# Down products of the channel mixers by Strassen's seven products over quarters, with pools of weights that begin and end with each phase

## The chip, the core and the metric

The kernel runs on one NeuronCore of a Trainium2 chip, as one program that leaves its output in HBM. What counts is the device time of one execution in microseconds (us). Engines: TensorE multiplies matrices (PE in the profile, PEld its weight loads), VectorE (DVE) and ScalarE (ACT) do elementwise work, GpSimd (POOL) almost nothing here, SyncE (SP) issues the transfers from HBM. TensorE writes its sums into PSUM, eight banks of 128 x 512 fp32 values; everything else lies in SBUF.

## The reference

A trunk of two layers over 512 tokens of 1024 features, fp32. Layer 0 has a chunked gMLP as its mixer (mixer A), layer 1 an RG-LRU (mixer B); each is followed by a gated ConvFFN, the channel mixer, whose last line is what the change rewrites:

```python
def conv_ffn(h, w_up, conv_w, conv_b, w_down):
    up = causal_dwconv(h @ w_up, conv_w, conv_b)
    gate, val = jnp.split(up, 2, axis=-1)
    return (jax.nn.gelu(gate) * val) @ w_down

    for i in range(DEPTH):
        h = rms_norm(x, norm_mix[i])
        ...
        h = rms_norm(x, norm_ffn[i])
        x = x + conv_ffn(h, f_w_up[i], f_conv_w[i], f_conv_b[i], f_w_down[i])
    return rms_norm(x, norm_final)
```

`w_up` is 1024 x 6144, `w_down` 3072 x 1024, and the depthwise convolution has three taps along the tokens.

## The kernel before

Activations lie feature-major: a tile is 128 features by 512 tokens, and `xall` keeps the eight tiles of `x`. The kernel keeps fp32 accuracy by splitting every operand into a high part, rounded to TensorE's fp32r format, and the exact rest, the low part. A product is then three matmuls that add up in PSUM, high by high, high by low and low by high (`mm3`, L99 to 103).

**Weights.** They stream from HBM in chunks of 512 KB, that is two tiles of 128 input rows by 512 output columns, 1024 values a partition. `load` (L93) issues the transfer into a `raw` buffer, and `split` (L85) makes the parts: ScalarE copies `raw` into `hi` (L89), VectorE subtracts for `lo` (L90), both at high priority. `raw`, `hi` and `lo` have three buffers each. Chunk names end in r, h and l: `fu000r` is the raw chunk of the first ConvFFN's up weights, block 0, chunk 0; `fu1..` belongs to the second ConvFFN, `fd0w..` and `fd1w..` to the down products, `aow..` to the output product of mixer A, `bx..` to the input product of mixer B.

**Blocks.** `block` (L106) takes four PSUM tiles, one for each 128 output features, and runs through the chunks of a weight; a chunk meets 24 matmuls of 512 columns. The up product of a ConvFFN is 12 such blocks of four chunks each. After each, VectorE multiplies the four tiles by the norm's scale (`up`, L468), ScalarE and VectorE convolve them (`conv`, L442 to 448; one step on ScalarE, two on VectorE), GELU and the gate make two tiles `cv`, and `to_parts` (L238) leaves their parts as `fy..`. After the 12 blocks the 24 tiles `fy` are the input of the down product: two column blocks of 512 output features, 12 chunks each. In layer 0 this is `project` (L245), in layer 1 `project_out` (L256), which also does the final norm and takes the last two chunks by halves of the tokens, with matmuls of 256 columns. `project` adds each finished tile to `xall` (L250) and makes the next norm's input at once: `norm_input` (ScalarE makes `xh`, L198; VectorE makes `xl`, L199), `square` (ScalarE `sq`, L207; VectorE adds it to `acc`, L208). The norm's scale itself is found later, by hooks that run after the first chunks of the next block.

**What sets the order.** The code is written in program order, and a tile scheduler puts each engine's instructions into a queue by priority and by what they depend on. The engine then works through its queue in that order and waits at each instruction for what it needs. The pools of buffers (`const`, `wp` for weights, `yp` for activations, `wk` for work tiles, `pp` for PSUM) are opened once and stay open for the whole program (L49 to 53).

Of the kernel before, what the change touches and what calls it, by code (L numbers as in the profile page):

```python
# [30 lines left out]
# Columns of the packed per-channel vectors.  # L31
# [13 lines left out]
def trunk(ctx: ExitStack, tc: tile.TileContext, xT, vecs, a_w_in, a_w_sT, a_b_s, a_w_out,  # L45
# [11 lines left out]

    def work(name="w"):
        return wk.tile([P, S], F32, tag="w", name=name)

    def work_r(name="wr"):
        return wk.tile([P, S], F32R, tag="w", name=name)

    def yhi(name="yh"):
        return yp.tile([P, S], F32R, tag="yh", name=name)

    def ylo(name="yl"):
        return yp.tile([P, S], F32R, tag="yl", name=name)

    # Activations whose tables differ, in the order of the program.  # L70
# [13 lines left out]
    # A chunk of a weight: 1024 values a partition, in two parts that add up to it exactly.  # L84
    def split(raw, shape, name):  # L85
        hi = wp.tile(shape, F32R, tag="hi", name=f"{name}h")
        lo = wp.tile(shape, F32R, tag="lo", name=f"{name}l")
        with tc.high_priority(HIGH):
            nc.scalar.copy(hi, raw)  # L89
            nc.vector.tensor_tensor(lo, raw, hi.bitcast(F32), op=ALU.subtract)  # L90
        return hi, lo

    def load(shape, parts, name):  # L93
        raw = wp.tile(shape, F32, tag="raw", name=f"{name}r")
        for sl, src in parts:
            nc.sync.dma_start(sl(raw), src)
        return split(raw, shape, name)
# [7 lines left out]
    # Feature-major product: one PSUM tile for each of four blocks of 128 output features.  # L105
    def block(kt, loader, acts, name, hooks={}):  # L106
        pss = [psum(f"{name}{m}") for m in range(4)]
        for kc in range(kt // 2):
            hi, lo = loader(kc)
            last = kc == kt // 2 - 1  # L110
            order = [(k, m) for m in range(4) for k in range(2)] if last else [(k, m) for k in range(2) for m in range(4)]
            for k, m in order:
                kk = 2 * kc + k
                w = (hi[:, k, m * P:(m + 1) * P], lo[:, k, m * P:(m + 1) * P])
                mm3(pss[m], w, acts[kk], kk == 0, kk == kt - 1)
            for hook in hooks.get(kc, ()):
# [16 lines left out]
    bs = const.tile([P, AG, P], F32, name="bs")  # L133
# [6 lines left out]
    # Keeps the tensor engine's clock up while the first loads are under way.  # L140
# [19 lines left out]
    # log of the sigmoid, by log1p(u) = 2 atanh(u / (2 + u)) with u = exp(-|lambda|)  # L160
# [54 lines left out]
    # The token's sum over the features, one token a partition.  # L215
# [6 lines left out]
    # The same scale along the free dimension, on all partitions.  # L222
# [21 lines left out]
    # A product back to the model's width, added to x; the next norm's input follows.  # L244
# [9 lines left out]
    # The last one, with the norm that ends the trunk. The last chunks of the second block go by halves  # L254
    # of the tokens, so that the first half leaves while the second is multiplied.
# [68 lines left out]
    xparts = list(zip(xh, xl))  # L324
# [10 lines left out]
    def first_chunk(kc, src):  # L335
        raw, hi, lo = (wp.tile([P, 2, 512], dt, tag=t, name=f"av0{kc}{t}") for dt, t in ((F32, "raw"), (F32R, "hi"), (F32R, "lo")))
# [10 lines left out]
    for fb in range(4):  # L347
# [24 lines left out]
        for c in range(NC):  # L372
            v = yp.tile([P, S], F32, tag="yl", name=f"vr{c}{fb}")
# [17 lines left out]
    # The lower triangle of the spatial weights, [s, g, t]: s <= t stays.  # L391
    wsr = wp.tile([P, AG, P], F32, tag="raw", name="wsr")
# [15 lines left out]
    # v's large part meets both parts of the weights side by side; the small products share one place.  # L408
# [23 lines left out]
    for mb in range(4):  # L432
        pss = block(KD, loader_of(a_w_in, mb * 512, f"au{mb}"), xparts, f"u{mb}", spatial_hooks(mb - 1) if mb else {})
        for m in range(4):
            ut = yp.tile([P, S], F32, tag="yl", name=f"u{4 * mb + m}")
# [14 lines left out]
    def conv_ffn(l, gain_name, gain_off):  # L450
        wu = f_w_up[l].rearrange("(k p) (two n) -> p k two n", p=P, two=2)
        yparts = []
        for b in range(NF // 2):
            def ld(kc):
                return load([P, 2, 2, 256], [
                    (lambda t, h=h: t[:, :, h, :], wu[:, 2 * kc:2 * kc + 2, h, b * 256:(b + 1) * 256]) for h in range(2)
                ], f"fu{l}{b}{kc}")

            def ld512(kc):
                hi, lo = ld(kc)  # L460
                return hi.rearrange("p k h n -> p k (h n)"), lo.rearrange("p k h n -> p k (h n)")
            pss = block(KD, ld512, xparts, f"f{b}", norm_hooks if b == 0 else {})
            for j in range(2):
                ts = []
                for half in range(2):
                    f = half * NF + 2 * b + j
# [6 lines left out]
                nc.vector.tensor_tensor(ts[1], ts[0], ts[1], op=ALU.mult)  # L473
                yparts.append(to_parts(ts[1], f"fy{2 * b + j}"))
        if gain_name is None:
            project_out(NF, f_w_down[l], yparts, f"fd{l}")
# [10 lines left out]
    def xb_block(mb, hooks={}):  # L487
        pss = block(KD, loader_of(b_w_in, BW + mb * 512, f"bx{mb}"), xparts, f"bx{mb}", hooks)
# [8 lines left out]
    def g_block(mb, hooks={}):  # L497
# [3 lines left out]
        for m in range(4):  # L501
            t = work("g0")
            nc.vector.tensor_tensor(t, pss[m], rbc, op=ALU.mult)
            g = yp.tile([P, S], F32, tag="yh", name=f"g{4 * mb + m}")
# [7 lines left out]
    # r, tanh(-log_a / 2) and i * xb  # L512
# [115 lines left out]
```

## Time and profile before

| | |
|---|---|
| Runs | 1341.81, 1341.93, 1341.54 us, median 1341.81 |
| Profiled execution, span from its first to its last instruction | 1339.3 us |
| Median of the runs less the span | 2.5 us |
| PE busy | 1329.0 us, 5862 matmuls |
| DVE busy | 802.6 us |
| ACT busy | 554.0 us |
| POOL busy | 12.0 us |
| HBM read | 126.11 MB |

The profile is of one execution. Busy time counts an engine's own work without its waits for others. A row of the timeline gives the start, the duration, the engine, the line of code, the operation, the output and its inputs; a bracket at its end tells how long the engine sat idle before it and whose end released it. Matmuls overlap: the time from one start to the next is what a matmul costs in a row of them, and the printed duration is longer.

### The profile page before, as it was taken

To read this page: it belongs to the slowest core of one execution; us is meant where nothing else is said; L and a number is where in the kernel's file an instruction comes from. 1 tells how busy PE (TensorE), PEld (TensorE's weight loads), DVE (VectorE), ACT (ScalarE), POOL (GpSimd) and SP (SyncE) were. 2 spreads that over 40 slices of the span, in tenths; PEclk is the share of its full clock that TensorE was granted. 3 is DMA by queue.
4 is the path that set the end of the run, shared out by engine and by line. 5 is a ranking of instruction groups with operands and counts; after the bars stand their busy time and mean duration, and the time that the engine had idled before them with its cause. 6 is when DMAs were issued, how large, how long until landed. Compare 5 with 4: busy or idle time off the path is not lost.

```text
span 1339.3 us, 15007 instructions
## 1 busy us (share of the span) xinstructions
PE 1329.0 (99%) x5862; PEld 1082.5 (81%) x5862; DVE 802.6 (60%) x1104; ACT 554.0 (41%) x743; POOL 12.0 (1%) x20
## 2 busy tenths in 40 slices
PE   9999999999999999999999999999999999999997
PEld 7888888888888888888888888888888888888886
DVE  7227775446767575724247799944676757572325
ACT  6455332333434343423233669633343434342322
POOL 1000000000000000000000000000000000000000
PEclk9999999999999999999999999999999999999999
DMA  6333222232222222232233323232222222223221
GB/s 230 94 94 109 80 79 94 94 95 94 94 95 90 94 90 92 94 105 98 94 94 95 95 79 95 97 108 94 95 94 95 90 94 90 92 93 105 99 79 64
DMA packets 96328, 129.19 MB, mean 96 GB/s; under 512 B 5888, under 2 KB 61184, under 8 KB 96256
## 3 DMA queue, kind: packets, MB, share of 16 engines
q1 hardware_dynamic: 96112, 128.22, 29.7%
q8 instruction: 46, 0.75, 0.2%
q14 instruction: 26, 0.21, 0.1%
q10 hardware_dynamic: 144, 0.00, 0.0%
HBM read 126.11 MB, written 2.10 MB: 96 GB/s over the span
## 4 chain that ended last, share of the span: by engine, by line
PE 98%; issue 0%; DMA 0%; DVE 0%; ACT 0%; DVEq 0%; POOLq 0%; POOL 0%
PE f L101 13%; PE f L102 13%; PE f L103 13%; PE fd0p L102 3%; PE fd0p L103 3%; PE fd0p L101 3%; PE fd1p L101 3%; PE fd1p L102 3%; PE fd1p L103 3%; PE u L101 2%; PE v L362 2%; PE v L363 2%; PE u L103 2%; PE u L102 2%; PE v L364 2%; PE aop L101 2%
## 5 line engine op out<-in xcount | busy, mean ns | idle before, releaser
L446 DVE SCALAR_TENSOR_TENSOR cv<-up,vt,cv 128x511 f32<-128x511 f32 (+1 forms) x192 | 140.8, 745 | 22.2 <-ACT cv L444 21.3
L444 ACT ACTIVATE cv<-up,vt 128x512 f32<-128x512 f32 x96 | 77.7, 812 | 77.3 <-DVE up L468 77.3
L468 DVE TENSOR_TENSOR up<-f,rbc 128x512 f32<-128x512 f32 x96 | 65.4, 683 | 0.2 <-issue 0.2
L473 DVE TENSOR_TENSOR cv<-cv 128x512 f32<-128x512 f32 x48 | 33.0, 688 | 1.0
L472 ACT ACTIVATE cv<-cv 128x512 f32<-128x512 f32 x48 | 30.2, 629 | 5.5 <-DVE cv L446 3.3
L198 ACT ACTIVATE xh<-xall,vt 128x512 fp32r<-128x512 f32 x24 | 17.2, 719 | 23.8 <-DVE xall L250 23.8
L422 DVE SCALAR_TENSOR_TENSOR sv<-sv,vt,bs 128x256 f32<-128x256 f32 x32 | 14.9, 477 | 19.1 <-PE sv L419 19.1
L207 ACT ACTIVATE sq<-xall 128x512 f32<-128x512 f32 (+1 forms) x37 | 21.7, 586 | 9.8 <-DVE xall L262 9.8
L446 DVE SCALAR_TENSOR_TENSOR xb<-xr,vt,xb 128x511 f32<-128x511 f32 (+2 forms) x36 | 25.5, 744 | 0.1
L208 DVE TENSOR_TENSOR acc<-acc,sq 128x512 f32<-128x512 f32 (+1 forms) x37 | 23.8, 642 | 2.0 <-ACT sq L207 1.9
L199 DVE SCALAR_TENSOR_TENSOR xl<-xall,vt,xh 128x512 fp32r<-128x512 f32 x24 | 17.9, 748 | 5.2 <-ACT xh L198 4.8
L213 POOL TENSOR_TENSOR rc<-ms,mhalf 128x4 f32<-128x4 f32 (+1 forms) x6 | 5.4, 905 | 1233.5 <-DVE ms L212 1233.5
L418 PE MATMUL sv<-ws,vh 128*128 128x256 f32 x64 | 15.4, 324 | 0.0
L424 DVE SCALAR_TENSOR_TENSOR sv<-sv,vt 128x256 f32<-128x256 f32 x32 | 15.0, 480 | 0.4
L419 PE MATMUL sv<-ws,vl 128*128 128x128 f32 x64 | 14.2, 222 | 0.0
L559 DVE TENSOR_TENSOR_SCAN hs<-riyh,sq 128x512 f32<-128x512 f32 x12 | 14.0, 1205 | 0.0
L76 ACT ACT_TABLE_LOAD x10 | 12.8, 1283 | 0.1
L419 PEld LDWEIGHTS sv<-ws,vl 128*128 128x128 f32 x64 | 12.2, 191 | 0.5
L418 PEld LDWEIGHTS sv<-ws,vh 128*128 128x128 f32 x64 | 12.1, 188 | 0.5
L437 ACT ACTIVATE u<-u 128x512 f32<-128x512 f32 x16 | 9.4, 625 | 7.1 <-DVE u L436 7.1
L444 ACT ACTIVATE xb<-xr,vt 128x512 f32<-128x512 f32 x12 | 9.8, 814 | 6.1 <-DVE xr L492 6.1
L388 DVE SCALAR_TENSOR_TENSOR vl<-vr,rv,vh 128x512 fp32r<-128x512 f32 x16 | 10.9, 747 | 1.9 <-ACT vh L387 1.9
(2590 smaller groups left out, 4210.9 us busy)
## 6 DMA issues: line engine op xcount, KB each, us to landing
xall<-xT SPq DMA_DIRECT2D x8, 256.0 KB, 5.0
outT<-o SPq DMA_DIRECT2D x8, 256.0 KB, 2.4
av00raw<-a_w_in SPq DMA_DIRECT2D x2, 256.0 KB, 3.7
av01raw<-a_w_in SPq DMA_DIRECT2D x2, 256.0 KB, 4.9
av02raw<-a_w_in SPq DMA_DIRECT2D x2, 256.0 KB, 5.7
av03raw<-a_w_in SPq DMA_DIRECT2D x2, 256.0 KB, 5.2
bs<-a_b_s SPq DMA_DIRECT2D x1, 512.0 KB, 6.0
av10r<-a_w_in SPq DMA_DIRECT2D x1, 512.0 KB, 6.5
```

Source lines behind the costliest of these rows:

```text
L101: nc.tensor.matmul(ps, wh, xh, start=first, stop=False)
L102: nc.tensor.matmul(ps, wh, xl, start=False, stop=False)
L103: nc.tensor.matmul(ps, wl, xh, start=False, stop=last)
L362: nc.tensor.matmul(pss[c], xh[kk][:, ts], hi[:, k, :], start=kk == 0, stop=False)
L363: nc.tensor.matmul(pss[c], xh[kk][:, ts], lo[:, k, :], start=False, stop=False)
L364: nc.tensor.matmul(pss[c], xl[kk][:, ts], hi[:, k, :], start=False, stop=kk == KD - 1)
L418: nc.tensor.matmul(ps[:, i], vh[:, ds_], w, start=True, stop=False)
L444: nc.scalar.activation(dst, src, AF.Identity, scale=col(wname, woff + last * wstep), bias=col(cname, coff))
L446: nc.vector.scalar_tensor_tensor(dst[:, i:], src[:, :S - i], col(wname, woff + (last - i) * wstep), dst[:, i:], op0=ALU.mult, op1=ALU.add)
L468: nc.vector.tensor_tensor(upt, pss[2 * half + j], rbc, op=ALU.mult)
L472: nc.scalar.activation(ts[0], ts[0], AF.Gelu_apprx_tanh)
L473: nc.vector.tensor_tensor(ts[1], ts[0], ts[1], op=ALU.mult)
```

## The change

**Seven products.** The 24 input tiles of a down product are taken as 12 pairs. For a pair, the weights of one column block of 256 + 256 output features are four quarters (two tiles of the pair by two output halves, 512 features apart), and the activations are four quarters (two tiles by two halves of the tokens, 256 each). Eight quarter products become seven of sums of quarters. `weight_sums` forms four sums of weight quarters on VectorE in three instructions and splits seven operands: part `a`, three raw quarters (768 values), and part `b`, the four sums (1024). `input_sums` forms four sums of the activations in three instructions and splits seven operands in one go (`y`, 7 x 256). `seven` multiplies: 7 products, 2 blocks of 128 output features, 3 matmuls of 256 columns each. Each of the seven products has a PSUM bank of its own and adds up there over the six pairs of a **round**.

**Rounds.** A down product is now two rounds of six pairs, the first after seven of the twelve up blocks, the second after the last. Each round has two column blocks (m = 0 and 1). At the end of each, `down` adds the seven banks to `xall` by eleven sums on VectorE and one copy on ScalarE (`e1`). In the second round of layer 0 `next_norm` follows, for four tiles at a time. In layer 1 only the first round goes this way; the second half of its down product stays plain, through `project_out` with half of the weights. Tiles are named by layer, first pair of the round and column block: `d060m` are the banks of layer 0, the round that begins with pair 6, column block 0; `d0616r` is the raw weight chunk of that round's column block 1, pair 6; `s` marks its sums, `ahi`, `alo`, `bhi`, `blo` the parts.

**Pools.** The pools `wp`, `yp` and `wk` end and begin with each phase: mixer A, ConvFFN 0, mixer B, ConvFFN 1. In the ConvFFNs `wp` has three raw buffers and four for high and for low parts, and a chunk of a round takes two of each; `y` has six buffers, `yr`, for the quarters before their split, one, `sm`, for the weight sums, one, and `wk` five instead of seven.

**Order of chunks.** The three `bx` blocks of mixer B take their chunks in the order 0, 2, 1, 3, since a column block of the rounds finishes tiles 0, 1, 4, 5.

```diff
-    wp = ctx.enter_context(tc.tile_pool(name="wp", bufs=3))
-    yp = ctx.enter_context(tc.tile_pool(name="yp", bufs=24))
-    wk = ctx.enter_context(tc.tile_pool(name="wk", bufs=7))
...
+    def enter(*pools):
+        stack = ExitStack()
+        for name, bufs in pools:
+            phase[name] = stack.enter_context(tc.tile_pool(name=name, bufs=bufs, reuse_waits="tile"))
+        return stack
...
+    PRODUCTS = ((1, 0, 0, 0), (2, 0, 2, 1), (4, 0, 1, 6), (6, 1, 2, 5), (7, 1, 0, 4), (5, 1, 1, 3), (3, 1, 3, 2))
...
+    def weight_sums(src, name):
+        raw = phase["wp"].tile([P, 4, 256], F32, tag="raw", name=f"{name}r", bufs=3)
...
+        with tc.high_priority(HIGH):
+            nc.vector.tensor_tensor(sums[:, 0:2], raw[:, 1:3], raw[:, 0:1].broadcast_to([P, 2, 256]), op=ALU.add)
+            nc.vector.tensor_tensor(sums[:, 2], raw[:, 1], sums[:, 1], op=ALU.add)
+            nc.vector.tensor_tensor(sums[:, 3], raw[:, 3], sums[:, 2], op=ALU.add)
+            for t, src in (("a", raw[:, 1:4]), ("b", sums)):
...
+                nc.scalar.copy(hi, src)
+                nc.vector.tensor_tensor(lo, src, hi.bitcast(F32), op=ALU.subtract)
...
+    def input_sums(raw, dst):
+        nc.vector.tensor_tensor(raw[:, 3:5], raw[:, 0:3:2], raw[:, 7:8].broadcast_to([P, 2, HS]), op=ALU.subtract)
+        nc.vector.tensor_tensor(raw[:, 5], raw[:, 3], raw[:, 2], op=ALU.add)
+        nc.vector.tensor_tensor(raw[:, 6], raw[:, 5], raw[:, 1], op=ALU.subtract)
+        hi, lo = dst[:, :, 0:HS], dst[:, :, HS:S]
+        nc.scalar.copy(hi, raw[:, 0:7])
+        nc.vector.tensor_tensor(lo, raw[:, 0:7], hi.bitcast(F32), op=ALU.subtract)
...
+    def seven(pairs, weight, name):
+        banks = {p[0]: psum(f"{name}m{p[0]}").rearrange("p (j t) -> p j t", j=2) for p in PRODUCTS}
+        for n, (q, x) in enumerate(pairs):
+            parts = weight_sums(weight(q), f"{name}{q}")
+            first, last = n == 0, n == len(pairs) - 1
+            for b, part, w, i in PRODUCTS:
+                hi, lo = parts[part]
+                for j in range(2):
+                    js = slice(j * P, (j + 1) * P)
+                    for m, (wt, xt) in enumerate(((lo, x[:, i, 0:HS]), (hi, x[:, i, 0:HS]), (hi, x[:, i, HS:S]))):
+                        nc.tensor.matmul(banks[b][:, j], wt[:, w, js], xt, start=first and j == 0 and m == 0,
...
+    def conv_ffn(l, gain_name, gain_off, chunks):
+        stack = enter(("wp", 4), ("y", 6), ("yr", 1), ("sm", 1), ("wk", 5))
...
+        def down(qs, then):
+            for m in range(2):
+                banks = seven([(q, ys[q]) for q in qs],
...
+                with tc.high_priority(HIGH):
+                    e1, u2, u3 = (etile(f"d{qs[0]}{m}{t}") for t in ("e1", "u2", "u3"))
+                    nc.scalar.copy(e1, banks[1])
+                    nc.vector.tensor_tensor(x1[:, :, t0], banks[2], x1[:, :, t0], op=ALU.add)
+                    nc.vector.tensor_tensor(x2[:, :, t0], x2[:, :, t0], banks[4], op=ALU.subtract)
+                    nc.vector.tensor_tensor(u2, banks[6], e1, op=ALU.subtract)
...
+        def next_norm(m):
+            for k in (2 * m, 2 * m + 1, 4 + 2 * m, 5 + 2 * m):
+                norm_input(k, col(gain_name, gain_off + k))
+                square(k)
+
+        half = NF // 4
+        for q in range(half + 1):
+            up(q)
+        down(list(range(half)), None)
+        for q in range(half + 1, NF // 2):
+            up(q)
+        if gain_name:
+            down(list(range(half, NF // 2)), next_norm)
         else:
-            project(NF, f_w_down[l], yparts, gain_name, gain_off, f"fd{l}")
-
-    conv_ffn(0, "norm_mix", KD)
+            project_out(NF // 2, f_w_down[l][half * 256:, :], plain, f"fd{l}")
+        stack.close()
+
+    mixer.close()
+    conv_ffn(0, "norm_mix", KD, None)
+    mixer = enter(("wp", 3), ("yp", 24), ("wk", 7))
...
-        pss = block(KD, loader_of(b_w_in, BW + mb * 512, f"bx{mb}"), xparts, f"bx{mb}", hooks)
+        pss = block(KD, loader_of(b_w_in, BW + mb * 512, f"bx{mb}"), xparts, f"bx{mb}", hooks, [0, 2, 1, 3])
...
-    conv_ffn(1, None, 0)
+    mixer.close()
+    conv_ffn(1, None, 0, None)
```

**How it moves instructions: ScalarE at the start of the first channel mixer.** In the queue before, the high parts of its first chunks (`fu000h`, `fu001h`) follow the last chunk of mixer A's output product (`aow17h`), ahead of the norm inputs and squares of that product's last four tiles:

```order
L89 CAST aow17h<-aow17r 128x1024
L89 CAST fu000h<-fu000r 128x1024
L89 CAST fu001h<-fu001r 128x1024
L198 ACTIVATE xh_76<-xall,vt 128x512
L207 ACTIVATE sq<-xall 128x512
L198 ACTIVATE xh_77<-xall,vt 128x512
L207 ACTIVATE sq<-xall 128x512
```

With the change they stand behind all of these (L210 and L219 are the new numbers of L198 and L207, L98 of L89):

```order
L98 CAST aow17h<-aow17r 128x1024
L210 ACTIVATE xh_67<-xall,vt 128x512
L219 ACTIVATE sq<-xall 128x512
L210 ACTIVATE xh_68<-xall,vt 128x512
L219 ACTIVATE sq<-xall 128x512
L210 ACTIVATE xh_69<-xall,vt 128x512
L219 ACTIVATE sq<-xall 128x512
L210 ACTIVATE xh_70<-xall,vt 128x512
L219 ACTIVATE sq<-xall 128x512
L98 CAST fu000h<-fu000r 128x1024
L98 CAST fu001h<-fu001r 128x1024
```

Both casts moved from ahead of eight steps to behind them. At the start of the second channel mixer the same two casts (`fu100h`, `fu101h`) moved alike.

**ScalarE at the start of mixer B,** with the change. The high part of its first chunk (`bx00h`) stands behind the last parts of the second round (`d06111..`), the copy of a bank (L569) that the round's last sums need, and the first norm input:

```order
L482 CAST d06111ahi<-d06111r 128x768
L482 CAST d06111bhi<-d06111s 128x1024
L569 COPY d61e_5713<-d061m_5364 128x512
L210 ACTIVATE xh_65<-xall,vt 128x512
L98 CAST bx00h<-bx00r 128x1024
L219 ACTIVATE sq<-xall 128x512
```

Before, `bx00h` and `bx01h` came right behind the last chunk of the down product, ahead of the first norm input.

**VectorE in the second round of the first channel mixer, at the turn** from column block 0 (banks `d060m`) to column block 1 (chunks `d0616` and on). These are the last four of the eleven sums, and what follows:

```order
L578 TENSOR_TENSOR xall<-xall,d60u_5333 128x2x256
L576 TENSOR_TENSOR xall<-d060m_4988,xall 128x2x256
L578 TENSOR_TENSOR xall<-xall,d60u_5333 128x2x256
L580 TENSOR_TENSOR xall<-xall,d60u_5332 128x2x256
L476 TENSOR_TENSOR d0616s<-d0616r 128x512
L483 TENSOR_TENSOR d0616alo<-d0616r,d0616ahi 128x768
L477 TENSOR_TENSOR d0616s<-d0616r,d0616s 128x256
L211 SCALAR_TENSOR_TENSOR xl_71<-xall,vt,xh_63 128x512
L478 TENSOR_TENSOR d0616s<-d0616r,d0616s 128x256
L211 SCALAR_TENSOR_TENSOR xl_72<-xall,vt,xh_64 128x512
L220 TENSOR_TENSOR acc<-acc,sq 128x512
L483 TENSOR_TENSOR d0616blo<-d0616s,d0616bhi 128x1024
```

All eleven sums stand ahead of the low parts of the new column block's first chunk, and between the two low parts come pieces of the next norm. None of these rows exists in the kernel before; there the low part of a down chunk (L90) is one row.

## Rows read from the trace of the kernel before

**Rows 1.** The page's part 1, busy time and share of the span.
```profile
PE 1329.0 (99%) x5862; PEld 1082.5 (81%) x5862; DVE 802.6 (60%) x1104; ACT 554.0 (41%) x743; POOL 12.0 (1%) x20
```

**Rows 2.** The chain that ended last, by engine and by line.
```profile
PE 98%; issue 0%; DMA 0%; DVE 0%; ACT 0%; DVEq 0%; POOLq 0%; POOL 0%
PE f L101 13%; PE f L102 13%; PE f L103 13%; PE fd0p L102 3%; PE fd0p L103 3%; PE fd0p L101 3%; PE fd1p L101 3%; PE fd1p L102 3%; PE fd1p L103 3%; PE u L101 2%; PE v L362 2%; PE v L363 2%; PE u L103 2%; PE u L102 2%; PE v L364 2%; PE aop L101 2%
```

**Rows 3.** Windows over ConvFFN 0's up and down products; columns as the first line says.
```profile
core 0: us, PE busy (x) PEld busy (x) DVE busy (x) ACT busy (x) POOL busy (x), PEclk, DMA share, GB/s
288.50:559.70 271.20, 271.20 (x1163) 218.23 (x1162) 182.20 (x241) 112.05 (x143) 1.01 (x1) 1.00 0.29 94
559.74:690.30 130.56, 130.56 (x577) 108.15 (x576) 47.48 (x53) 36.26 (x43) 0.00 (x0) 1.00 0.30 97
```

**Rows 4.** Timeline of PE in the last chunks, 256 columns: start, duration, operation.
```profile
1315.63 0.28 PE L101 MATMUL fd1p<-fy20h,fd1w110h 128*128 128x256 f32 x1
...
1321.38 0.28 PE L101 MATMUL fd1p<-fy20h,fd1w110h 128*128 128x256 f32 x1
```

**Rows 5.** Timeline at the start of ConvFFN 0: ScalarE, TensorE and VectorE.
```profile
277.60 1.05 ACT L89 CAST fu000h<-fu000r 128x1024 fp32r<-128x1024 f32 x1 [4.38 <-PE aop L102]
...
288.51 0.40 PE L101 MATMUL f<-xh,fu000h 128*128 128x512 f32 x1
...
288.97 0.39 PE L103 MATMUL f<-xh,fu000l 128*128 128x512 f32 x1
...
289.29 0.68 DVE L250 TENSOR_TENSOR xall<-aop,xall 128x512 f32<-128x512 f32 x1
...
292.99 0.72 ACT L198 ACTIVATE xh<-xall,vt 128x512 fp32r<-128x512 f32 x1 [1.75 <-DVE xall L250]
293.62 0.62 ACT L207 ACTIVATE sq<-xall 128x512 f32<-128x512 f32 x1
294.15 1.04 ACT L89 CAST fu003h<-fu003r 128x1024 fp32r<-128x1024 f32 x1
```

**Rows 6.** Timeline of VectorE, and one row of ScalarE, around the last up blocks.
```profile
541.09 0.68 DVE L473 TENSOR_TENSOR cv<-cv 128x512 f32<-128x512 f32 x1
541.69 0.74 DVE L446 SCALAR_TENSOR_TENSOR cv<-up,vt,cv 128x510 f32<-128x510 f32 x1
...
561.11 1.23 DVE L90 TENSOR_TENSOR fd0w02l<-fd0w02r,fd0w02h 128x1024 fp32r<-128x1024 f32 x1
562.25 1.40 DVE L446 SCALAR_TENSOR_TENSOR cv<-up,vt,cv 128x510 f32<-128x510 f32 x2
...
564.17 0.74 DVE L446 SCALAR_TENSOR_TENSOR cv<-up,vt,cv 128x510 f32<-128x510 f32 x1
564.83 0.69 DVE L468 TENSOR_TENSOR up<-f,rbc 128x512 f32<-128x512 f32 x1
...
569.33 0.69 DVE L473 TENSOR_TENSOR cv<-cv 128x512 f32<-128x512 f32 x1
...
570.05 0.62 ACT L240 CAST fy23h<-cv 128x512 fp32r<-128x512 f32 x1 [2.75 <-DVE cv L473]
```

**Rows 7.** Groups by form, VectorE, L262: count, busy us, mean ns.
```profile
L262 DVE TENSOR_TENSOR xall<-fd1p,xall 128x256 f32<-128x256 f32 x8 | 3.4, 424 | 2.2 <-PE fd1p L103 1.8
```

**Rows 8.** Windows at the end (columns of rows 3), and two rows of PE's timeline.
```profile
1329.00:1332.50 3.50, 1.16 (x8) 1.04 (x8) 2.13 (x5) 0.93 (x2) 0.70 (x1) 1.00 0.63 218
1332.50:1333.00 0.50, 0.37 (x2) 0.00 (x0) 0.09 (x1) 0.00 (x0) 0.00 (x0) 0.84 0.93 342
1333.00:1334.00 1.00, 0.00 (x0) 0.00 (x0) 1.00 (x2) 0.00 (x0) 0.00 (x0) 0.50 0.18 65
...
1.26 4.19 PE L145 MATMUL warm<-warm 128*128 128x512 bf16 x10 [1.26 <-DVE warm L142]
...
1332.17 0.70 PE L285 MATMUL rb<-dg,ones_f 128*128 128x256 f32 x2 [1.49 <-DVE dg L278]
```

**Rows 9.** One weight chunk's transfer, issue to landing.
```profile
DMA to landing us min/median/max: 2.8/3.0/3.1
```

More of the change, by code (lines that the diff above doesn't have):

```diff
@@ L103, in mm3, with block @@
         nc.tensor.matmul(ps, wl, xh, start=False, stop=last)
-    def block(kt, loader, acts, name, hooks={}):
+    def block(kt, loader, acts, name, hooks={}, chunks=None):
         pss = [psum(f"{name}{m}") for m in range(4)]
-        for kc in range(kt // 2):
+        for n, kc in enumerate(chunks or range(kt // 2)):
             hi, lo = loader(kc)
-            last = kc == kt // 2 - 1
+            last = n == kt // 2 - 1
             order = [(k, m) for m in range(4) for k in range(2)] if last else [(k, m) for k in range(2) for m in range(4)]
@@ L114, in block @@
                 w = (hi[:, k, m * P:(m + 1) * P], lo[:, k, m * P:(m + 1) * P])
-                mm3(pss[m], w, acts[kk], kk == 0, kk == kt - 1)
-            for hook in hooks.get(kc, ()):
+                mm3(pss[m], w, acts[kk], n == 0 and k == 0, last and k == 1)
+            for hook in hooks.get(n, ()):
                 hook()
@@ L138, in load_x @@
         nc.sync.dma_start(xs[k], xT[k * P:(k + 1) * P, :])
+    mixer = enter(("wp", 3), ("yp", 24), ("wk", 7), ("bs", 1))
+    bs = phase["bs"].tile([P, AG, P], F32, name="bs")
     warm = work("warm").bitcast(BF16)[:, 0:S]
@@ new lines, in halves @@
+    def halves(t):
+        return t.rearrange("p (h t) -> p h t", h=2)
+    def seven(pairs, weight, name):
[9 more added lines that the diff above has]
+                        nc.tensor.matmul(banks[b][:, j], wt[:, w, js], xt, start=first and j == 0 and m == 0,
+                                         stop=last and j == 1 and m == 2, skip_group_check=True)
+        return banks
@@ L451, in conv_ffn, with etile, up @@
+    def etile(name):
+        return phase["wk"].tile([P, 2, HS], F32, tag="w", name=name)
+    def conv_ffn(l, gain_name, gain_off, chunks):
+        stack = enter(("wp", 4), ("y", 6), ("yr", 1), ("sm", 1), ("wk", 5))
         wu = f_w_up[l].rearrange("(k p) (two n) -> p k two n", p=P, two=2)
-        yparts = []
-        for b in range(NF // 2):
+        wd = f_w_down[l].rearrange("(k p) (two n) -> p k two n", p=P, two=2)
+        ys, plain = {}, []
+        summed = NF // 2 if gain_name else NF // 4
+        def up(q):
@@ L454, in ld @@
             def ld(kc):
[L455 to L460, printed above, removed]
+                hi, lo = load([P, 2, 2, 256], [
+                    (lambda t, h=h: t[:, :, h, :], wu[:, 2 * kc:2 * kc + 2, h, q * 256:(q + 1) * 256]) for h in range(2)
+                ], f"fu{l}{q}{kc}")
@@ L461, in ld512 @@
                 return hi.rearrange("p k h n -> p k (h n)"), lo.rearrange("p k h n -> p k (h n)")
-            pss = block(KD, ld512, xparts, f"f{b}", norm_hooks if b == 0 else {})
+            pss = block(KD, ld, xparts, f"f{q}", norm_hooks if q == 0 else {}, chunks)
+            y = phase["y"].tile([P, 7, S], F32R, tag="y", name=f"y{q}")
+            if q < summed:
+                raw = phase["yr"].tile([P, 8, HS], F32, tag="yr", name=f"yr{q}")
             for j in range(2):
@@ L465, in conv_ffn @@
                 for half in range(2):
[L466 removed]
+                    f = half * NF + 2 * q + j
                     upt = work("up")
```

78 lines of the change are left out of this document (55 added, 23 removed).

## Prediction

> **What bounds the kernel now.** I read the engine totals first: TensorE is busy 99% of a span of 1339.3 us, VectorE 60%, ScalarE 41% [rows 1]. The chain that ended last says the same from the other end, 98% of it is PE and nearly all of that the three matmul lines of `mm3` [rows 2]. So time goes or comes in two ways only: another sum of matmul durations, or a wait of TensorE that today is not there. The windows show where cover exists: through the up products of the first channel mixer VectorE works 182 of 271 us, through the down product that follows only 47 of 131 [rows 3]. The change puts its new work into that second stretch.
>
> **Matmuls.** Of the three halves it rewrites, each loses 12 x 8 x 3 = 288 matmuls of 512 columns and gets 6 pairs x 2 column blocks x 7 products x 2 x 3 = 504 of 256. A 512-column matmul of the down product costs 130.56 us / 576 = 0.2267 us [rows 3]. For 256 columns the end of the kernel has the nearest rows: 48 of them, each with a weight load of its own, lie between the starts 1315.63 and 1321.38, so 0.1198 us each [rows 4], more than half of 0.2267. Out: 864 x 0.2267 = 195.8 us. In: 1,512 x 0.1198 = 181.1 us. **-14.7 us**: of the eighth that seven products save, more than a third goes to shorter matmuls. The rows of the seven products also use one weight twice running, as `mm3` does, so I see no reason for another rate.
>
> **Three starts that lose their cover.** The pools of weights now end and begin with each phase, and in the built order the first weight chunk of a phase is split only behind the last tiles' norm work: on ScalarE `fu000h` stands behind the last square, where before it stood ahead of all eight of these steps; so also at the second channel mixer, and `bx00h` at mixer B. Today the split of `fu000` runs ten us early, at 277.60, and the up products begin at 288.51 without a wait [rows 5]. With the new order I walk the rows from there. VectorE adds the third tile at 289.29 [rows 5] and now the fourth right behind (back to back, 512 elements start every 0.60 us: 541.09 to 541.69 [rows 6]), done at 290.5. ScalarE meanwhile does two norm inputs and two squares, starting every 0.63 and 0.53 us (292.99, 293.62, 294.15 [rows 5]), from 290.0 to 292.35; then `fu000h`, 1.05 us, to 293.4; then `fu000l` on VectorE, 1.23 us, to 294.65. TensorE's third matmul needs it, and today starts at 288.97 [rows 5]: a wait of 5.7 us. Mixer B's start, behind the last sums of the second round, comes to 5.5 us by the same steps. Nothing else stands in TensorE's queue. Three times 5.6: **+16.8 us**. Lower end, if nothing were ahead of the last tile: 0.2 (a matmul's end behind its successor's start) + 0.69 + 0.72 + 0.62 + 1.05 + 1.23 - 0.47 = 4.05, three times 12.2; upper end 18.
>
> **VectorE in the rounds.** A weight chunk of a round costs VectorE 512 + 256 + 256 elements of sums and 768 + 1024 of low parts. By the rows: 0.60, twice 0.34 (0.424 long [rows 7], 0.085 less back to back, as for 512), 0.87 (768, between the rows of 512 and 1024), 1.14 (561.11 to 562.25 [rows 6]): 3.3 us. TensorE takes 42 x 0.1198 = 5.03 us for it. Alone this fits: with the wait for ScalarE's high part between (1.05 us; a hand-over is 0.03 us, 570.02 to 570.05 [rows 6]) the chain is 4.7 us. But six chunks, 19.7 us of VectorE in 30.2 us, share it with the convolutions of the next up block (4 x 0.60 + 8 x 0.66 + sums and split of its output, 12 us), and then with eleven sums out of PSUM (6.6 us) and, in the second round, the norm input as well. And high and low parts have buffers for two chunks only, so VectorE can't work ahead. What it owes shows at the turn from the first column block to the second:
> - Second round of the first mixer. All eleven sums stand ahead of the first low part of block two. They can start when product 2 of the last chunk is done, 3.4 us before the turn, and with two waits on their own results take 6.8 us; then 0.60 + 0.87: TensorE waits 4.9 us. The second low part comes 3.74 us later, behind two `xl` and an `acc`; the 18 matmuls that don't need it last 2.16 us: 1.6 more. Next chunk 0.8 more. 7.3 us.
> - First round, first mixer. The first low part is ahead of the sums, the second behind eight of them: 1.1 us; next chunk 0.35 us; and behind that stands the 7 x 256 low part of `y6`, 2.0 us (1024 elements 1.23, so 1792 some 2.04), which waits until TensorE frees the buffer: 2.5 us. 4.0 us.
> - First round, last mixer: `y6` is plain there and the second low part earlier: 2.7 us.
> Together **+14.0 us**. Lower end 5.2: the second round's order alone, with VectorE free at the instant the last product ends (four rows and the first low part, 3.65, then 1.6). Upper end 22: all waits half as long again. The last chunk of each round, the turn back to up blocks and the plain half cost nothing: their splits stand ahead of the sums.
>
> **The clock.** TensorE's grant is 1.00 in all windows of the run but the last: it reads 0.84 from 1332.5 and 0.50 from 1333, after 3.5 us in which TensorE did 1.16 us of work [rows 8]. Ten warm-up matmuls at the start take 4.19 us, 0.42 each, which is the lower of the two levels (1.2 of 2.4 GHz) [rows 8]: a fall costs some 4.2 x (1 - 0.2267/0.42) = 1.9 us at the next start. Four waits of some 5 us: nothing, if none falls; 7.7 us, if all do. The nearest row fell after 3.5 us that were partly busy, yet no row has TensorE idle for 5 and then at work, so I take near the middle, **+3.5 us**.
> The Trainium skill ("TensorE: Matmul & The Clock Gate", section "Why this matters for your kernels") tells authors to leave no long idle stretch between bursts of matmuls, since the clock then halves. By that rule all four waits would fall and the sum would be 4.2 us larger; the end of this trace agrees, and no row here shows it in mid-kernel.
>
> DMA: bytes stay the same, in rows of 1 KB as the up weights have them today; a chunk lands in 3.0 us [rows 9] against 5.03 us of work and three buffers. Nothing. The block order 0, 2, 1, 3 in mixer B moves no wait: its later inputs are ready 13 us after the turn and wanted at 16.
>
> **Sum.** -14.7 + 16.8 + 14.0 + 3.5 = +19.6 us, on the profiled span of 1339.3: 1358.9 us. The runs' median, 1341.81, lies 2.5 us above the span, so **1361.4 us**.
>
> **Rivals.**
> - *The slower matmuls of the normed inputs speed up.* 1,152 matmuls of an up phase take at most 271.20 us, 0.2354 each, against 0.2267 of the down product, with no wait and the same grant [rows 3]. If that comes of where `xh` and the weights lie, the new pools could end it. Worth (271.20 - 261.2) x 2 = 20 us in the mixers' up products and 12 more in 1,344 others: 1329.4 us. It would have to bring 22 of these 32 us to be faster than before. Against it: `xh` stays where it is and the weights move by 4 KB. 0.05.
> - *The turns cost only what their order forces*: 12.2 + 5.2 - 14.7 = +2.7, no fall of the clock: 1344.5 us. For it: VectorE's 3.3 of 5.03 us leave room; against: buffers for two chunks. 0.10.
> - *The clock falls in every wait*: 7.7 in place of 3.5: 1365.6 us. For it the last windows [rows 8]; against: a gap of 1.49 us near the end did nothing by itself [rows 8]. 0.20.
> - *VectorE's chain sets the rounds*: 4.7 us against 5.03 leaves 0.33 over five hand-overs. At 0.15 us each the chain is 5.3, 0.27 more on some 30 chunks, 8 us, and turns a fifth longer, 3: 1372 us. 0.13.
> - That the change doesn't do what it says is out: the built order has the 1,512.
>
> **Numbers.** The forecast itself, 1361.4, has 0.52. The range 1345 to 1374 takes in the second to the fourth rival but for the edge and the bounds of the waits. 0.2% is 2.7 us, what a measurement of this kernel can tell (its runs spread over 0.4 us). Faster by more: the first rival, 0.05. Within: half of the second, 0.05. Slower: 0.90.
>
> **What would show it.** Right: TensorE's busy time down, but idle before the first matmul on `fu000`, `fu100` and `bx00` of 4.7 us each with the rest before the third; idle on `L514` at the first chunks of each second column block, longest on `d0616`; starts of 256-column matmuls 0.12 us apart; a grant below 1.00 behind the waits. Wrong: the first matmuls of a phase at once behind the last, or rounds of 60 us without idle time, or a chunk that steadily takes more than 5.03 us.

## The result and the profile after

The changed kernel takes 1365.96 us (median of 4 runs, 1364.13 to 1366.57) against 1341.69 us: a ratio of 1.0179, 95% interval 1.0166 to 1.0191. The forecast was 1361.4, within 1345 to 1374. The profiled execution is the 1364.13 us one; its span is 1362.4 us, 23.1 more than before. It is the shortest of the four; the others read a mean clock grant of 0.986 against its 0.989, so the clock's term below may be larger in them.

The page of the changed kernel, parts 1 and 4, answers to [rows 1] and [rows 2]:

```profile
PE 1327.4 (97%) x6510; PEld 1108.9 (81%) x6510; DVE 956.7 (70%) x1342; ACT 591.0 (43%) x767; POOL 12.1 (1%) x20
...
PE 90%; DVE 6%; issue 2%; ACT 1%; DVEq 0%; POOLq 0%; POOL 0%; ACTq 0%
```

TensorE has 648 more matmuls and is busy for hardly less time, and the chain now runs through VectorE and ScalarE for some 7% of the span. Where, the waits of TensorE tell (who waited for what, us in total, times, longest):

```profile
PE d061m L514 <- DVE d0616alo L483: 5.0, 1, 5.0
PE bx L110 <- ACT bx00h L98: 4.6, 1, 4.6
PE f L110 <- ACT fu100h L98: 4.5, 1, 4.5
PE f L110 <- ACT fu000h L98: 4.5, 1, 4.5
PE d001m L514 <- DVE d0011blo L483: 2.5, 1, 2.5
...
PE d101m L514 <- DVE d1011blo L483: 1.2, 1, 1.2
PE d101m L514 <- DVE d1011alo L483: 1.2, 1, 1.2
PE d001m L514 <- DVE d0010blo L483: 1.2, 1, 1.2
```

Three starts of phases, three turns between column blocks, nothing else new. The windows price them (columns as in [rows 3]). Each window runs from the first matmul of a block to the first of the next:

```profile
293.67:319.28 25.61, 25.57 (x107) 20.27 (x107) 12.86 (x18) 8.00 (x10) 1.01 (x1) 0.94 0.44 144
454.23:484.46 30.23, 30.23 (x253) 30.23 (x252) 27.16 (x43) 13.01 (x16) 0.00 (x0) 1.00 0.22 70
484.46:519.19 34.73, 30.97 (x255) 30.39 (x253) 28.75 (x40) 14.32 (x16) 0.00 (x0) 1.00 0.34 107
631.63:667.12 35.49, 30.54 (x253) 30.23 (x251) 32.47 (x49) 15.92 (x20) 0.00 (x0) 0.98 0.20 60
667.12:704.55 37.43, 32.84 (x253) 32.64 (x253) 31.31 (x48) 14.79 (x20) 0.00 (x0) 0.91 0.28 85
704.55:759.22 54.67, 54.63 (x227) 43.61 (x227) 39.74 (x55) 23.31 (x31) 1.01 (x1) 0.95 0.35 106
946.36:973.16 26.80, 26.76 (x106) 21.16 (x107) 12.86 (x18) 8.00 (x10) 1.01 (x1) 0.89 0.43 138
1108.11:1138.35 30.24, 30.24 (x254) 30.23 (x252) 26.35 (x40) 14.14 (x17) 0.00 (x0) 1.00 0.25 78
1138.35:1171.55 33.20, 30.75 (x254) 30.34 (x253) 27.62 (x42) 12.76 (x15) 0.00 (x0) 1.00 0.33 105
```

A column block of a round with no wait takes 30.23 us (second row), which is 252 matmuls of 0.120. The blocks behind the three turns take 34.73, 37.43 and 33.20, and the one ahead of the second round's turn 35.49, since the wait lies at its end. The first, sixth and seventh row are the first blocks of the channel mixers and the first stretch of mixer B. In the kernel before the same stretches took 23.82, 51.94 and 23.83 us at a grant of 1.00 (the column PEclk: the share of TensorE's full clock that it was granted):

```profile
288.51:312.33 23.82, 23.82 (x107) 19.35 (x106) 13.91 (x22) 8.53 (x12) 1.01 (x1) 1.00 0.27 89
690.30:742.24 51.94, 51.94 (x228) 41.94 (x227) 37.70 (x54) 20.98 (x27) 1.01 (x1) 1.00 0.31 91
924.71:948.54 23.83, 23.83 (x108) 19.34 (x107) 13.77 (x21) 8.27 (x11) 1.01 (x1) 1.00 0.28 89
```

Why they are longer, though each starts only after its wait, two windows at the second channel mixer show, the wait and what follows it:

```profile
941.67:946.36 4.69, 0.16 (x1) 0.00 (x0) 4.50 (x9) 3.36 (x6) 0.00 (x0) 0.91 0.00 2
946.36:952.30 5.94, 5.90 (x13) 4.21 (x14) 3.48 (x4) 2.81 (x3) 0.00 (x0) 0.50 0.53 168
```

TensorE stands still for 4.69 us (the windows begin where the last matmul's 0.2267 us end; by the printed ends it is 4.5), its grant falls, and it then works for 5.94 us at 0.50, the lower of the two levels. So it is behind all four long waits: the grant was 0.51, 0.51, 0.50 and 0.50 in the windows of 3.3 to 5.9 us that follow them.

The sum, in us of span:

| term | forecast | measured | from |
|---|---|---|---|
| matmuls of the rounds | -14.7 | -14.5 | 6 x 30.23 for 130.56 + 65.28 (half of 576 x 0.2267) |
| three starts, up to the first matmul | +16.8 (with the wait for the first low part) | +14.1 | 3 x 4.69 |
| three turns | +14.0 | +15.2 | 4.50; 5.26 + 2.51; 2.97 |
| behind the starts: low clock and first low part | +3.5 (clock alone, four waits) | +7.5 | 1.79 + 2.73 + 2.97 |
| elsewhere | 0 | +0.8 | the rest to 23.1; 0.5 of it before 98 us |

The 2.51 is what is left of 37.43 - 30.23 when the 4.69 us that TensorE waits for `bx00h` are counted with the starts.

### The profile page after: what moved, and what is told of

The parts are those of the page before. It is cut to its first block, busy times and chain, and to the rows that moved or that the text cites. A ratio compares the mean times of both kernels' runs of the same rounds, so it can differ in the third digit from the quotient of the medians.

```text
span 1362.4 us, 16705 instructions
## 1 busy us (share of the span) xinstructions
PE 1327.4 (97%) x6510; PEld 1108.9 (81%) x6510; DVE 956.7 (70%) x1342; ACT 591.0 (43%) x767; POOL 12.1 (1%) x20
## 4 chain that ended last, share of the span: by engine, by line
PE 90%; DVE 6%; issue 2%; ACT 1%; DVEq 0%; POOLq 0%; POOL 0%; ACTq 0%
PE f L110 13%; PE f L112 13%; PE f L111 13%; PE v L373 2%; PE u L110 2%; PE v L374 2%; PE u L112 2%; PE u L111 2%; PE d061m L514 2%; PE v L375 2%; PE aop L110 2%; PE aop L111 2%; PE aop L112 2%; PE d001m L514 2%; PE bx L110 2%
## 5 line engine op out<-in xcount | busy, mean ns | idle before, releaser
L457 DVE SCALAR_TENSOR_TENSOR cv<-up,vt,cv 128x511 f32<-128x511 f32 (+1 forms) x192 | 140.5, 745 | 24.4 <-ACT cv L455 23.1
L494 DVE TENSOR_TENSOR y<-yr,y 128x1792 fp32r<-128x1792 f32 x18 | 36.4, 2024 | 5.7 <-ACT y L493 5.7
L210 ACT ACTIVATE xh<-xall,vt 128x512 fp32r<-128x512 f32 x24 | 17.2, 716 | 48.6 <-DVE xall L262 35.7
L493 ACT CAST y<-yr 128x1792 fp32r<-128x1792 f32 x18 | 30.4, 1690 | 5.5 <-PE d001m L514 5.5
L219 ACT ACTIVATE sq<-xall 128x512 f32<-128x512 f32 (+1 forms) x37 | 21.7, 586 | 15.2 <-DVE xall L274 15.2
L550 DVE TENSOR_TENSOR yr<-cv 128x512 f32<-128x512 f32 x36 | 24.7, 686 | 0.6
L554 ACT CAST y<-cv 128x512 fp32r<-128x512 f32 x12 | 7.3, 620 | 29.3 <-DVE cv L552 23.6
L262 DVE TENSOR_TENSOR xall<-aop,xall 128x512 f32<-128x512 f32 x8 | 5.4, 685 | 10.9 <-PE aop L112 10.8
L262 DVE TENSOR_TENSOR xall<-bop,xall 128x512 f32<-128x512 f32 x8 | 5.4, 685 | 10.8 <-PE bop L112 10.8
```

Of the source, the lines that this page charges most:

```text
L457: nc.vector.scalar_tensor_tensor(dst[:, i:], src[:, :S - i], col(wname, woff + (last - i) * wstep), dst[:, i:], op0=ALU.mult, op1=ALU.add)
L493: nc.scalar.copy(hi, raw[:, 0:7])
L494: nc.vector.tensor_tensor(lo, raw[:, 0:7], hi.bitcast(F32), op=ALU.subtract)
```

## Experiments

**e1: the pools alone.** The kernel before, with its plain products:

```diff
+    pools = (("wp", 3), ("yp", 24), ("wk", 7))
+    stack = enter(*pools)
...
+    stack.close()
+    stack = enter(*pools)
     conv_ffn(0, "norm_mix", KD)
+    stack.close()
+    stack = enter(*pools)
```

> The kernel before, with plain down products, in which only the pools of weights, activations and work tiles end and begin with each phase. Theory (the three starts cost what they cost because the first chunk's split stands behind the last norm work): the same three waits of 4.7 us before the first matmul of both channel mixers and of mixer B, and 1.8 to 3 us behind each while the clock is low, 21 us in all: 1363 us, with a rise at the three starts alone. Rival (it is the lag of VectorE after the new sums that holds the starts, and pools alone cost little): 1342 to 1346 us.

1364.97 us, a ratio of 1.0171 (1.0156 to 1.0186). The waits are those of the three starts and no others:

```profile
PE f L105 <- ACT fu100h L93: 4.5, 1, 4.5
PE bx L105 <- ACT bx00h L93: 4.5, 1, 4.5
PE f L105 <- ACT fu000h L93: 4.5, 1, 4.5
```

The first block of the first channel mixer takes 26.69 us behind its wait, 2.87 more than before; the other two starts lose 2.93 and 3.09 in the same way. 3 x 4.69 + 8.9 = 23.0 us. The theory gave 1363 us, the rival 1342 to 1346. Closing the pools, without one of Strassen's products, costs 23.1 us, nearly as much as the whole change (24.3).

**e2: the reverse.** The changed kernel with weights in one pool that stays open:

```diff
-    mixer = enter(("wp", 3), ("yp", 24), ("wk", 7), ("bs", 1))
+    weights = enter(("wp", 3))
+    mixer = enter(("yp", 24), ("wk", 7), ("bs", 1))
...
-        stack = enter(("wp", 4), ("y", 6), ("yr", 1), ("sm", 1), ("wk", 5))
+        stack = enter(("wx", 1), ("y", 6), ("yr", 1), ("sm", 1), ("wk", 5))
...
+        return phase["wp" if turn[0] % 4 else "wx"]
```

> The changed kernel with one pool of weights (three buffers of each kind) open for the whole program, and the fourth high and low buffers of the channel mixers in a pool of their own, taken in the same rotation; all else as changed. Theory: first chunks are split ahead of the norm work again, the three waits and the low clock behind them go, 21.6 us: 1344 us, up to 1347 if mixer B's start keeps a rest from VectorE. Rival (the split is early but TensorE waits as long for xh of the last tiles or for VectorE): 1360 us or more.

1340.94 us, 0.9995 of the kernel before (0.9985 to 1.0004), 25 us less than the change and 3 less than the theory gave. The split is early again, where [rows 5] had it:

```profile
277.49 1.05 ACT L107 CAST fu000h<-fu000r 128x1024 fp32r<-128x1024 f32 x1 [4.38 <-PE aop L120]
```

No wait is left at any start, mixer B's among them. What is left are turns, and the second round's has become one of 6.7 us. So the products and their turns cancel each other almost exactly.

**e3: the next column block's first chunk ahead of the sums,** in the changed kernel:

```diff
+                if m == 0:
+                    ahead = weight_sums(wd[:, 2 * qs[0]:2 * qs[0] + 2, :, 256:512], f"d{l}{qs[0]}1{qs[0]}")
```

> The changed kernel with one edit: the first chunk of a round's second column block gets its sums and parts in program order ahead of the eleven sums out of the banks. Theory (at the turn of the second round only VectorE's order holds TensorE): the wait of 5.0 us there goes to under 1, and with it the low clock behind it, 2 us; the first rounds gain 1 us each: 1357 to 1360 us. Rival (VectorE owes the work anyway, so that the wait moves from the first chunk to the second): 1363 to 1366 us, with a wait on the second chunk in its place.

1364.53 us, the rival. The wait of 5.0 us went to 0.8, and others came:

```profile
PE d001m L514 <- DVE d0011blo L483: 2.9, 1, 2.9
PE d061m L514 <- DVE d0617alo L483: 1.9, 1, 1.9
...
PE d061m L514 <- DVE d0617blo L483: 1.3, 1, 1.3
```

The second round gains 1.8 us in all (31.33 + 39.83 against 35.49 + 37.43), the first round loses 1.9 (36.60 against 34.73; the grant was 0.95 in that window). Order alone moves the wait to the next chunk. The 1.4 us between the medians lie within the spread of the two kernels' runs.

**e4: the clock held up.** Matmuls of a zero tile fill the four waits:

```diff
+    def idle_fill(n):
+        b = filler
+        fill = psum("fill")
+        for i in range(n):
+            nc.tensor.matmul(fill, b[:, 0:P], b, start=i == 0, stop=i == n - 1)
...
+    idle_fill(18)
     mixer.close()
```

> The changed kernel with 18 matmuls of a zero tile (bf16, 512 columns, some 4 us) for TensorE in each of its four waits of 5 us, their sums left unused; with them in the queue, the first matmuls of a phase come high parts first, so that the wait for the first low part is hidden too. Theory (the clock falls in each of the four waits and costs 2 to 3 us behind each, 9 to 11 us in all, not the 3.5 of the forecast): 1355 to 1357 us, a grant of 1.00 throughout, with the waits themselves unchanged in length. Rival (the clock costs some 3.5 us, the rest lies in the waits): 1362 us. Second rival (the clock falls for another reason than the idle time): 1366 us and the low grants still there.

1357.9 us (1356.32 to 1359.17), 8.1 less than the change, nearer the theory than the first rival. In the profiled execution, the one of 1356.32 us, the grant stays at 1.00 in all these places. Its mean grant is 0.998; two of the four executions, of 1359.0 and 1359.2 us, read 0.995, so the clock was probably not held in all of them. The wait and the first block of the first channel mixer, then the first block of the second:

```profile
288.83:293.30 4.47, 3.83 (x17) 1.57 (x17) 4.28 (x8) 3.36 (x6) 0.00 (x0) 1.00 0.00 0
293.30:317.23 23.93, 23.93 (x106) 19.46 (x107) 12.86 (x18) 8.01 (x10) 1.01 (x1) 1.00 0.48 154
...
941.85:965.79 23.94, 23.94 (x107) 19.46 (x108) 12.87 (x18) 8.02 (x10) 1.01 (x1) 1.00 0.49 154
```

The waits are as long as they were; the blocks behind them are back at 23.9. The three starts give 7.2 us. Part of that can be the first low part, whose wait the high-parts-first order hides here; the low part's 1.23 us less the 0.47 of the first two matmuls are 0.8 us a start at most, so at least 4.8 is the clock in this execution. The turn of the second round gives nothing (68.55 us for its two blocks with the start's wait left out, 68.23 in the changed kernel): there TensorE waits again, 1.4 us, for the second low part, which the slow matmuls had hidden.

**e8: the turns without their sums.**

```diff
-                with tc.high_priority(HIGH):
+                if m:
+                  with tc.high_priority(HIGH):
                     e1, u2, u3 = (etile(f"d{qs[0]}{m}{t}") for t in ("e1", "u2", "u3"))
```

> The changed kernel without the eleven sums and the bank copy at the end of the first column block of each round (four of the eight tiles of x get nothing from these rounds; the second column block's sums stay). Theory (the turns are held by those sums): the excess over 30.23 us goes at all three turns, 4.5 + 5.3 + 2.5 + 3.0 us with the low clock behind them, and the starts keep theirs: 1350 to 1353 us. Rival (VectorE is late anyway, from the convolutions of the next up block and buffers for two chunks): the turns of the two first rounds keep 2 to 3 us each: 1355 to 1358 us.

This kernel leaves out what the rounds add to four of the eight tiles of `x`. 1349.94 us, as the theory has it. The blocks behind the first two turns, and the one behind the third:

```profile
485.00:515.24 30.24, 30.24 (x255) 30.24 (x253) 24.56 (x34) 13.41 (x14) 0.00 (x0) 1.00 0.40 127
...
657.91:688.21 30.30, 30.30 (x254) 30.20 (x252) 22.28 (x32) 9.93 (x12) 0.00 (x0) 1.00 0.35 105
1126.64:1156.88 30.24, 30.24 (x254) 30.24 (x253) 23.34 (x34) 12.86 (x15) 0.00 (x0) 1.00 0.39 125
```

All three excesses are gone. Without the sums neither the convolutions nor buffers for two chunks hold TensorE; the starts keep their 4.5 to 4.6 us.

**e5: the next norm out of the turn,** on top of e2:

```diff
-                if then:
-                    then(m)
+            for m in range(2 if then else 0):
+                then(m)
```

> The kernel of e2 (one pool of weights) with the next norm's inputs of the first four tiles placed behind the second column block of the round, not at the turn. Theory (at that turn TensorE waits 6.7 us for the second low part, which on VectorE stands behind the sums and three pieces of the norm, and on ScalarE behind four; then at the low clock): the wait falls to 2 us or less and the low clock behind it goes: 1333 to 1335 us, below the kernel before. Rival (VectorE owes the same work whatever its order; the waits move to the next chunks): 1339 us or more.

1338.68 us, 0.9977 (0.9967 to 0.9986): faster than both kernels, but by less than the theory has it, and next to the rival's 1339. The wait of 6.7 us went to 2.7, and one of 1.7 us came at the third chunk: two `xl` of the norm stand on VectorE ahead of its sums and between them (665.46 and 666.73 us).

**e6: four sums on GpSimd.** Those that read no bank (`nc.gpsimd` for `nc.vector` in the last three statements of `down`):

> The kernel of e5 with four of the eleven sums at the end of a column block, those that read no bank of PSUM, on GpSimd instead of VectorE (2.4 us of VectorE at each turn). Theory (what is left of the turns is VectorE's lag): the rests of 2.9 and 2.2 us at the turns of the two first rounds halve and the second round's goes under 1: 3 us less than e5, 1331 us. Rival (GpSimd is slow at this, or slows VectorE beside it, and the norm inputs that follow the last round come later): as e5 or up to 5 us more, with a wait at mixer B's start.

1340.45 us, 1.8 more than e5: the rival. On VectorE such a sum starts every 0.60 us; on GpSimd:

```profile
L590 POOL TENSOR_TENSOR xall<-xall,d01u 128x512 f32<-128x512 f32 x4 | 7.1, 1791 | 3.5 <-DVE d01u L585 3.5
...
L591 POOL TENSOR_TENSOR xall<-xall,d00e 128x512 f32<-128x512 f32 x2 | 2.6, 1300 | 346.4 <-DVE xall L582 346.4
```

1.3 to 2.1 us each by the profile, whose spans on GpSimd are rough, and TensorE waits 1.2 us for the norm's last `acc` in mixer B, which it didn't in e5.

**e7: the seventh pair's split behind the round:** `input_sums` for `y6` called after `down`.

> The kernel of e5 with the sums and the split of the seventh pair's activations of the first channel mixer (y6, its low part alone 2.0 us of VectorE) behind the first round in program order. Theory (that low part sits among the first chunks after the turn of that round): 1 to 1.5 us less than e5, the turn of d001 alone. Rival (it fills time in which VectorE would wait): no difference from e5 beyond 0.5 us.

1338.69 us, e5 to the hundredth, and it tells nothing of `y6`: in the built order that low part did not move. VectorE has it at 484.96 us, ahead of `d0011blo`, as in e5 at 485.06. What `y6` costs at this turn is read from the changed kernel's trace alone, below.

**e9: the same four sums at normal priority on VectorE,** for the first column block of each round, on top of e5.

> The kernel of e5 with the four of the eleven sums that read no bank of PSUM at normal instead of high priority at the end of the first column block, so that three to four of them follow the next chunk's sums and parts on VectorE. Theory (the rests at the turns are VectorE's work ahead of the next parts, 2.4 us of it movable): 1.5 us less at each of the three turns: 1334 to 1336 us. Rival (what is left comes of buffers for two chunks: the parts can't start earlier): 1338 us, as e5.

1336.0 us, 0.9958 (0.9944 to 0.9972), 2.7 less than e5, as the theory has it in sum. By turns it is not, which leaves the theory's 1.5 us a turn unconfirmed: the first rounds' blocks fall from 33.17 to 32.17 and from 32.47 to 30.85, the second round keeps its wait.

**e10: e9 with the edit of e3.**

> The kernel of e9 with the edit of e3 as well (the first chunk of a round's second column block ahead of the sums out of the banks in program order); on VectorE its second low part moves ahead of two of the sums. Theory (the wait of 2.8 us for that low part, at the turn of the second round, is those two rows): 1.2 us less there: 1334.8 us. Rival (as in e3, what is gained at the first chunk is lost at the second): 1336 us.

**1334.02 us**, 0.9942 (0.9928 to 0.9955): the fastest kernel of this study, 7.7 us below the one before and 32 below the change. The wait at the second round's turn is 1.6 us. What gained 1.4 us in e3, within its spread, gains 2.0 here, and all of it in the second round; the first rounds' blocks are as in e9 (32.17 and 30.85). That it pays because the sums and the norm can now give way is a reading of the order; no run tests it alone, and e9's profile has the clock low behind this wait where e10's has not.

**e11: what a short matmul costs.** e10 with each 256-column matmul of the rounds cut into two of 128.

> The kernel of e10 with each 256-column matmul of the rounds cut into two of 128 columns with the same weights, each with its own weight load: the same sums. It prices a shorter matmul. If the spacing of 0.120 us is set by columns (0.0567 us for 128, as a quarter of 0.2267), a column block stays near 30 us and the time near 1334. If a weight load of its own each sets it (the loads leave no gap in the rounds), 128 columns cost 0.120 as well: 60 us a column block, 1334 + 6 x 30 = 1515 us. Between: a fixed part and a part for columns.

1484.14 us (one run). A column block without waits:

```profile
448.17:504.40 56.23, 56.23 (x506) 56.23 (x504) 33.68 (x50) 14.51 (x17) 0.00 (x0) 1.00 0.17 52
```

56.23 us / 504 = 0.1116 us for 128 columns, against 0.120 for 256 and 0.2267 for 512. Neither pure theory: below 256 columns a matmul with a weight load of its own hardly gets cheaper. Whether the load or the matmul's own fixed part sets the 0.11 this run doesn't tell apart.

## Why the prediction was right, and where it was off

**Matmuls: right.** -14.5 for -14.7. The 0.1198 us from the end of the kernel [rows 4] held for all 1,512: 0.120. The rival that the matmuls of the normed inputs speed up failed: an up block takes 22.49 us in both kernels.

**Three starts: the mechanism right, and nearly the size.** 4.7 us of idle time before the first matmul were forecast; the waits are 4.5 to 4.6. The walk from [rows 5] holds step by step; behind VectorE's last addition ScalarE does two norm inputs and squares, then the split:

```profile
290.31 0.72 ACT L210 ACTIVATE xh<-xall,vt 128x512 fp32r<-128x512 f32 x1 [1.88 <-DVE xall L262]
290.94 0.61 ACT L219 ACTIVATE sq<-xall 128x512 f32<-128x512 f32 x1
291.46 0.70 ACT L210 ACTIVATE xh<-xall,vt 128x512 fp32r<-128x512 f32 x1
292.07 0.61 ACT L219 ACTIVATE sq<-xall 128x512 f32<-128x512 f32 x1
292.59 1.03 ACT L98 CAST fu000h<-fu000r 128x1024 fp32r<-128x1024 f32 x1
```

The transfer of `fu000r` is no rival: it was issued by 269.9 us and took at most 3.8. e1 shows that the pools alone make these waits, e2 that a pool of weights that stays open removes them. The further 0.9 us a start, the wait for `fu000l`, came too, though TensorE's matmuls show no wait for it: the load of its weights waits 0.8 us, and the third matmul starts 0.81 us later than two of 0.2267 behind the first would let it.

```profile
293.67 0.80 PE L110 MATMUL f<-xh,fu000h 128*128 128x512 f32 x1 [4.53 <-ACT fu000h L98]
294.26 0.63 PE L111 MATMUL f<-xl,fu000h 128*128 128x512 f32 x1
294.93 0.80 PE L112 MATMUL f<-xh,fu000l 128*128 128x512 f32 x1
```

At the low clock the two matmuls ahead last nearly as long as that split, so these 0.81 us, the same at the other two starts, can be put down to the low part or to the clock. Counted with the low part, as the forecast does, the starts cost 14.1 + 2.4 = 16.5 us for 16.8.

**Three turns: right.** 7.8, 4.5 and 3.0 us for 7.3, 4.0 and 2.7. VectorE does what the order said at the second round's turn, and `d0616alo` comes after the last sum:

```profile
658.89 0.68 DVE L570 TENSOR_TENSOR xall<-d060m,xall 128x512 f32<-128x512 f32 x1
...
664.92 0.68 DVE L580 TENSOR_TENSOR xall<-xall,d60u 128x512 f32<-128x512 f32 x1
665.52 0.68 DVE L476 TENSOR_TENSOR d0616s<-d0616r 128x512 f32<-128x512 f32 x1
666.13 0.95 DVE L483 TENSOR_TENSOR d0616alo<-d0616r,d0616ahi 128x768 fp32r<-128x768 f32 x1
```

TensorE waits 4.96 us there, 4.9 forecast. The forecast's 1.6 us for the second low part is not there as a wait: the 18 matmuls ahead of it run at the low clock, 4.0 us (667.12 to 671.14) in place of 2.16, and hide it. With the clock held up (e4) the wait comes out, 1.4 us, so the 2.51 us behind the turn come to the same either way. At the first round's turn the part put down to `y6`, 2.5 us, came as well: its low part waits for ScalarE, which waits for TensorE to free the buffer, and `d0011blo` stands behind it:

```profile
492.84 2.03 DVE L494 TENSOR_TENSOR y<-yr,y 128x1792 fp32r<-128x1792 f32 x1 [0.93 <-ACT y L493]
494.79 1.22 DVE L483 TENSOR_TENSOR d0011blo<-d0011s,d0011bhi 128x1024 fp32r<-128x1024 f32 x1
```

TensorE's wait for `d0011blo` is 2.5 us, that for `d0010blo` 1.2 where 1.1 was forecast. Yet the sums ahead of it are needed too: without them (e8) the same low part runs at 492.24 us, one chunk later, and TensorE waits for nothing. What it costs by itself no run here separates. The forecast's reason, VectorE in debt, is right with one limit: the debt is made at the turn itself, and the convolutions before it alone leave none that shows. The rival by which the turns cost only what their order forces, 5.2 us, is out; so is VectorE's chain, since 30.23 us without a wait leaves no room for it.

The sum's upper end for the turns, "half as long again", is 21 us by its own terms, not 22; nothing hangs on it.

**The clock: the term that was mis-sized.** The step was "so I take near the middle, +3.5 us", between no fall and four. All four waits made the grant fall. The fourth fall cost nothing, because VectorE held the turn anyway (e4). The other three and the first low parts together cost 7.5 us in the profiled run and 8.9 in e1; less 2.4 for the low parts that is 5.1 and 6.5, or 1.7 to 2.2 us a fall, and e4 gives 4.8 at least. So the 1.9 us for one fall was near, though the low clock lasted 3.3 to 5.9 us of work and not the 4.2 of the ten matmuls of [rows 8]; what was wrong is the count, some two falls where three cost something. The forecast's likeliest case was not the one that came: the mechanism of its third rival was, the clock falling in every wait, given 0.20. That its 1365.6 us is so near to 1365.96 is partly luck: it has four falls at 1.9 us, 7.7, where three at 5.1 came, and turns and the rest of the program made up 2.0. The Trainium skill ("TensorE: Matmul & The Clock Gate", section "Why this matters for your kernels") tells authors to leave no long idle stretch between bursts of matmuls; the trace agrees, with 0.50 behind 4.69 us without work.

## What to carry to other kernels

On a kernel that is 98% one engine, price a change by the waits it opens on that engine, not by the work it saves: here seven products for eight saved 14.5 us, and a change of pools that looked like housekeeping cost 23. A buffer pool that is closed between phases takes away the early preparation of the next phase; keep what feeds the bound engine open across the seam, and read the new order of the engines that prepare it. Where one engine holds a seam, moving one of its tasks forward only moves the wait (e3): first let give way what nobody waits for (e5, e9), then move the urgent part ahead (e10).

## What the runs showed of the hardware that was not expected

- TensorE's grant fell in every wait of 4.5 us and more in the middle of the program that no matmuls filled. At waits of about 3 us executions differ. Behind 2.9 us in e3 (`d0011blo`), and behind 3.1 in e6, 2.7 in e7 and 2.8 in e9 (`d0616blo`), the profiles read 0.50; behind 2.7 us in e5 and 2.5 in the changed kernel they read 1.00.
- e5 and e7 had the same wait there, 2.75 and 2.74 us. In the same window behind it (e5 first, then e7) the clock stayed in one and fell in the other, and the two kernels' times are the same. Where VectorE holds the next chunks, a fall costs nothing: TensorE waits 1.7 us for the third chunk in e5 and 0.5 in e7.

```profile
658.50:662.00 3.50, 3.42 (x27) 3.21 (x28) 3.50 (x7) 3.09 (x5) 0.00 (x0) 1.00 0.03 11
658.50:662.00 3.50, 3.50 (x22) 3.50 (x22) 3.50 (x7) 3.08 (x5) 0.00 (x0) 0.64 0.00 1
```

- Eighteen matmuls of a tile of zeros (4.5 us) kept the grant at 1.00 in the profiled execution of e4.
- A matmul with a weight load of its own costs 0.2267, 0.120 and 0.1116 us at 512, 256 and 128 columns. A second level of seven products would turn four matmuls of 256 columns into seven of 128: by these figures, as an estimate, 0.78 us for 0.48, so it would cost time.
